# Which PSUM bank the second head's transposed probabilities use, and which head norm starts one block later

## The chip, the cores and the metric

The kernel runs on one core of one Trainium2 chip. The number that counts is the device time of one execution in microseconds (us); smaller is better. Engines are named as in the profile: PE is TensorE (matmuls and transposes), PEld its weight loads, ACT is ScalarE, DVE is VectorE, POOL is GpSimd, SP issues the weight transfers. PSUM, where PE writes its results, has eight banks; a tile here is always one whole bank.

## The reference, cut to what matters

The model is two blocks over 256 tokens of width 1024: an even mixer, an expert layer, an attention layer with 16 heads of 64 (`fox_mix`), a second expert layer, then a second block with a windowed attention of 8 heads (`sliding_window_attention`) and a gated MLP. The change touches the two attentions only.

```
q = rms_norm(q.reshape(B, S, FOX_HEADS, FOX_HD), q_g)     # the head norm; k likewise
k = rms_norm(k.reshape(B, S, FOX_HEADS, FOX_HD), k_g)
...
logits = logits + c[:, :, lo:hi, None] - c[:, :, None, :hi]   # c: cumulated log of the forget gates
probs = jax.nn.softmax(jnp.where(mask, logits, -jnp.inf), axis=-1)
outs.append(jnp.einsum('bhqk,bhkd->bhqd', probs.astype(v.dtype), v[:, :, :hi]))
```

## The kernel before, in words

Each engine executes its instructions in the order in which the program issues them. All weights come as a stream of blocks of 128 x 1024 numbers. SP fetches a block (`w_raw`), ACT makes its high part (`w_hi`, L337), DVE the remainder (`w_lo`, L353), and PE multiplies with both. A weight block is 24 matmuls of 256 columns or 12 of 512.

Small work is woven between the blocks by generators that yield: `flow.step()` advances every active generator by one step, oldest first. In the attention `attend` (L1410) makes one round of it: one step, one weight block, then a new pair of heads is added, then two more steps. `pair_chain` (L1350) is the generator of one pair of heads. Its steps are: logits of head 0 with row maximum and exponential; the same for head 1; division by the row sums (L1384, L1387, which write `pb`); the transposes of head 0's probabilities (`pt`, L1393) and the copy out of PSUM (`pts`, L1395); the same for head 1; an empty step; the product with the values (`po`, L1403); and the split of that product into `y_hi` (ACT) and `y_lo` (DVE, L1406, shown in the trace as L460 and L461; `ya_hi` and `ya_lo` in the second block). Since a new pair starts in every round, three pairs are under way at once. In one round the order on PE is: block, `po` of the oldest pair, head 0's transposes of the middle pair, head 0's logits of the newest, head 1's transposes of the middle pair, head 1's logits of the newest, next block.

The four objects `pj`, `pa`, `pl` and `po` each hand out PSUM banks in turn from a list. While the pairs run the lists are

```
banks((4, 5), (0,), (1, 2), (3,))        # pj, pa, pl, po in fox_mix
banks((4, 5, 6, 7), (0,), (1, 2), (3,))  # in the windowed attention
```

so that `pa` has bank 0 and `po` has bank 3. A tile that is put into a bank waits until the tile before it in that bank has been read.

Ahead of the pairs, while the q and k blocks of `fox_mix` are multiplied, `quad(b)` (L1515) norms four tiles at a time by `rms_heads` (L1314): step 1 sums squares with matmuls of 2 columns (`qn_ps`), takes a root on ACT and an inverse on DVE; steps 2 and 3 spread the result by transposes (`qn_rb`). There are four of these, `quad(0)`, `quad(2)`, `quad(4)` and `quad(6)`. `forget()` (L1448) runs beside them: a projection with 16 outputs (`fz_ps`), then ACT work with three table loads (Exp, Ln, Sqrt), then the sums `c_ps`. A bare `yield` ahead of a quad puts it one weight block later.

Of the kernel before, what the change touches and what calls it, by code (L numbers as in the profile page):

```python
# [378 lines left out]
def body(ctx: ExitStack, tc: tile.TileContext, a, out, phases=(0, 6)):  # L379
# [20 lines left out]
    pj, pa, pl, po = Banks(), Banks(), Banks(), Banks()  # L400
# [26 lines left out]
    def col(name, i=0, n=1):  # L427
        at, w = COLS[name]
        assert i + n <= w
        return cols[:, at + i:at + i + n]  # L430
# [20 lines left out]
    def mm(o, l, r, start, stop):  # L451
        nc.tensor.matmul(o, l, r, start=start, stop=stop, skip_group_check=True)  # L452
# [6 lines left out]
    def split_to(hi, lo, src):  # L459
        nc.scalar.activation(hi, src, AF.Copy)  # L460
        nc.vector.tensor_sub(lo, src, hi.bitcast(F32))  # L461

    def preload(func):

        nc.scalar.activation(scr, epst, func)
# [848 lines left out]
    def rms_heads(qk, qz, sq, items, gains, tp, bd64, bufs=2):  # L1314


        n = len(items)
        ps = pa("qn_ps")
        ind = bd64[:, 0:P:64]
        for i, b in enumerate(items):  # L1320
            for tb in range(2):
                j = 4 * i + 2 * tb
                mm(ps[:, j:j + 2], sq(b)[:, tb * P:(tb + 1) * P], ind, i + tb == 0, True)
        rs = tp.tile([P, 4 * n], F32, name="qn_rs", tag="qn_rs")
        nc.scalar.activation(rs, ps[:, :4 * n], AF.Sqrt, bias=epst, scale=1.0 / 64)
        nc.vector.reciprocal(rs, rs)
        rx = tp.tile([P, 4 * n, 64], F32, name="qn_rx", tag="qn_rx", bufs=bufs)
        nc.scalar.activation(rx, rs.unsqueeze(2).to_broadcast([P, 4 * n, 64]), AF.Copy)
        yield
        for i0 in range(0, n, 2):  # L1330
            m = min(2, n - i0)
            hb = pa("qn_rb")
            for i in range(i0, i0 + m):
                for tb in range(2):
                    j = 4 * i + 2 * tb
                    nc.tensor.transpose(hb[:, ((i - i0) * 2 + tb) * P:((i - i0) * 2 + tb + 1) * P],
                                        rx[:, j:j + 2].rearrange("p a b -> p (a b)"), ident)
            for i in range(i0, i0 + m):
                b = items[i]
                at = slice((i - i0) * S, (i - i0 + 1) * S)  # L1340
                if b >= qz.shape[2]:
                    nc.vector.scalar_tensor_tensor(qk(b), qk(b), gains[i], hb[:, at], op0=OP.mult, op1=OP.mult)
                    continue
                for e in range(2):
                    pr = slice(e * 64, (e + 1) * 64)
                    nc.vector.scalar_tensor_tensor(qz[pr, e, b], qk(b)[pr], gains[i][pr], hb[pr, at],
                                                   op0=OP.mult, op1=OP.mult)
            yield

    def pair_chain(b, heads, tp, qz, kT, y, bias, shift, sink, vcol, vn, ready):  # L1350

        lts, mxs, pbs, ptss = [], [], [], []
        for e, hd in enumerate(heads):
            lg = pl("lg")
            lt = [lg[:, S:S + P], lg[:, 0:S]]
            for tb in (1, 0):
                n = (tb + 1) * P
                mm(lt[tb], qz[:, e, b, tb * P:n], kT[:, 0:n], tb == 1, False)  # L1360
            bias(hd, lg[:, 0:S + P])
            mx = tp.tile([P, 6], F32, name="mx", tag="mx", bufs=6)
            pb = tp.tile([P, 3, P], F32, name="pb", tag="pb", bufs=5)
            pbt = [pb[:, 0], pb[:, 1:3].rearrange("p a b -> p (a b)")]
            sk = sink(hd)
            for tb in range(2):
                nc.vector.tensor_reduce(mx[:, tb:tb + 1], lt[tb], axis=AX.X, op=OP.max, negate=sk is None)
            for tb in range(2):
                m = mx[:, tb:tb + 1]
                if sk is None:  # L1370
                    nc.vector.tensor_scalar(m, m, shift(hd)[tb], shift(hd)[tb], op0=OP.subtract, op1=OP.add)
                else:
                    nc.vector.tensor_scalar(m, m, sk, -1.0, op0=OP.max, op1=OP.mult)
            for tb in range(2):
                nc.scalar.activation(pbt[tb], lt[tb], AF.Exp, bias=mx[:, tb:tb + 1], accum_out=mx[:, 2 + tb:3 + tb])
            if sk is not None:
                nc.scalar.activation(mx[:, 4:6], mx[:, 0:2], AF.Exp, bias=sk)
            mxs.append(mx)
            pbs.append((pb, pbt))
            yield  # L1380
        for mx, (pb, pbt), hd in zip(mxs, pbs, heads):
            if sink(hd) is not None:
                nc.vector.tensor_add(mx[:, 2:4], mx[:, 2:4], mx[:, 4:6])
            nc.vector.reciprocal(mx[:, 2:4], mx[:, 2:4])  # L1384
        for mx, (pb, pbt) in zip(mxs, pbs):
            for tb in range(2):
                nc.vector.tensor_scalar(pbt[tb], pbt[tb], mx[:, 2 + tb:3 + tb], None, op0=OP.mult)  # L1387
        yield
        for e, hd in enumerate(heads):

            pt = (po if e else pa)("pt")
            for j in range(3):
                nc.tensor.transpose(pt[:, j * P:(j + 1) * P], pbs[e][0][:, j], ident)  # L1393
            pts = tp.tile([P, 3, P], F32, name="pts", tag="pts", bufs=4)
            nc.scalar.activation(pts.rearrange("p a b -> p (a b)"), pt[:, :3 * P], AF.Copy)  # L1395
            ptss.append(pts)
            yield
        yield
        ps = po("po")

        for j, (tb, kb) in enumerate(((0, 0), (1, 0), (1, 1))):
            for e, hd in enumerate(heads):
                mm(ps[e * 64:(e + 1) * 64, tb * P:(tb + 1) * P], vn[:, kb, vcol(hd):vcol(hd) + 64],  # L1403
                   ptss[e][:, j], j == 0, j != 1)
        yield
        split_to(y[0][:, b], y[1][:, b], ps[:, :S])  # L1406
        ready.add(b)
        yield
# [16 lines left out]
    def odd():  # L1425
        banks((4, 5, 6, 7), (0, 1, 2, 3))
        with ExitStack() as es:
# [85 lines left out]
            ready = set()  # L1513

            def quad(b):  # L1515
                if b == 0:
                    yield
                yield from rms_heads(lambda b: qk[:, b], qz, lambda b: sq[:, slot(b)], [b, 8 + b, b + 1, 9 + b], [gq, col("odk"), gq, col("odk")], tp, bd64)
                if b == 6:
                    preload(AF.Exp)  # L1520
                    for bb in range(8):
                        pending.append(pair_chain(bb, (2 * bb, 2 * bb + 1), tp, qz, qk[:, 8 + bb], y, bias,
                                                  lambda hd: [cq[:, tb, hd:hd + 1] for tb in range(2)],
                                                  lambda hd: None, lambda hd: hd * 64, vn, ready))

            def qk_out(b, ps):
                nc.vector.tensor_mul(qk[:, b], ps[:, :S], rb)
                nc.scalar.activation(sq[:, slot(b)], qk[:, b], AF.Square)
                if b >= 8 and b % 2:
                    flow.add(quad(b - 9))  # L1530
# [318 lines left out]
```

## Time and profile before

| | |
|---|---|
| three timed runs, median | 2374.05 us (2372.49 to 2374.91) |
| profiled execution, its own time | 2373.32 us |
| its span in the profile | 2371.5 us |
| PE busy | 2316.3 us, 98% of the span |
| PE clock granted, mean over the span | 0.991 of full speed |
| DVE, ACT busy | 73%, 57% |
| mean memory traffic | 163 GB/s |

PE is busy nearly all of the time, so what PE waits for is what can be won or lost; the few slices of the page in which PE falls below 9 tenths are the stages with attention. Its busy time also holds stretches in which its clock was granted at half.

### The profile page before, as it was taken

Reading aid. Unit: us, or ns where it says so; the run is one execution under the profiler, and the core shown is the slowest. Engines: PE = TensorE matmul, PEld = TensorE weight load, DVE = VectorE, ACT = ScalarE, POOL = GpSimd, SP = SyncE. Lnnn points to the kernel's source line nnn. Section 1 sums busy time; section 2 is a strip of 40 time slices with the busy share of each in tenths; the row PEclk is TensorE's granted clock in tenths of the full one; section 3 lists DMA queues with packets and bytes.
Section 4 is the critical chain, followed back from the end, with each engine's and each line's share of the span. In section 5 each row is a group of like instructions: output and inputs, shape, how many; then the busy total and the mean of one; then the engine's idle time right before and its main releaser. Section 6 shows DMA issues by size and latency. Waiting matters only on the chain. (4 is left out here: it accounts for less than half of the span.)

```text
span 2371.5 us, 48790 instructions
## 1 busy us (share of the span) xinstructions
PE 2316.3 (98%) x19664; PEld 2267.2 (96%) x19664; DVE 1723.1 (73%) x3656; ACT 1361.4 (57%) x2488; POOL 81.1 (3%) x99
## 2 busy tenths in 40 slices
PE   8999999999999999998899999999999999989999
PEld 7889999999999999997799999999999999989999
DVE  6768989999655555555489899996555555657983
ACT  6236448888544444555464588885444445555762
POOL 4100000000000000000000000000000000000200
PEclk9999999999999999999999999999999999999999
DMA  6125654444566666552155554445556565645563
GB/s 212 54 67 179 194 185 152 146 146 140 184 187 184 203 185 186 169 185 96 48 169 194 180 156 146 143 143 184 184 187 203 186 187 161 213 126 173 180 185 124
DMA packets 106627, 386.82 MB, mean 163 GB/s; under 512 B 11960, under 2 KB 13273, under 8 KB 106017
## 3 DMA queue, kind: packets, MB, share of 16 engines
q1 hardware_dynamic: 104976, 377.99, 50.6%
q0 software_dynamic: 1136, 5.32, 0.7%
q8 instruction: 154, 2.52, 0.4%
q14 instruction: 73, 0.59, 0.1%
q10 hardware_dynamic: 288, 0.40, 0.1%
HBM read 383.40 MB, written 1.05 MB: 162 GB/s over the span
## 5 line engine op out<-in xcount | busy, mean ns | idle before, releaser
L353 DVE TENSOR_TENSOR w_lo<-w_raw,w_hi 128x1024 fp32r<-128x1024 f32 x710 | 866.1, 1224 | 383.7 <-ACT w_hi L337 382.2
L337 ACT ACTIVATE w_hi<-w_raw 128x1024 fp32r<-128x1024 f32 x710 | 745.7, 1054 | 433.9 <-PE pv L452 348.6
L452 PE MATMUL pu<-h_hi,w_hi 128*128 128x256 f32 x2048 | 586.8, 287 | 0.0
L452 PE MATMUL pu<-h_lo,w_hi 128*128 128x256 f32 x2048 | 575.2, 281 | 0.0
L452 PE MATMUL pu<-h_hi,w_lo 128*128 128x256 f32 x2048 | 574.6, 281 | 0.0
L452 PE MATMUL pv<-h_hi,w_hi 128*128 128x256 f32 x1888 | 530.4, 281 | 0.0
L452 PE MATMUL pv<-h_lo,w_hi 128*128 128x256 f32 x1888 | 530.4, 281 | 0.0
L452 PE MATMUL pv<-h_hi,w_lo 128*128 128x256 f32 x1888 | 530.4, 281 | 0.0
L452 PEld LDWEIGHTS pu<-h_lo,w_hi 128*128 128x128 f32 x2048 | 386.4, 189 | 0.0
L452 PEld LDWEIGHTS pu<-h_hi,w_lo 128*128 128x128 f32 x2048 | 385.7, 188 | 0.0
L452 PEld LDWEIGHTS pu<-h_hi,w_hi 128*128 128x128 f32 x2048 | 385.5, 188 | 0.0
L452 PEld LDWEIGHTS pv<-h_hi,w_lo 128*128 128x128 f32 x1888 | 355.8, 188 | 0.0
L452 PEld LDWEIGHTS pv<-h_lo,w_hi 128*128 128x128 f32 x1888 | 355.8, 188 | 0.0
L452 PEld LDWEIGHTS pv<-h_hi,w_hi 128*128 128x128 f32 x1888 | 355.8, 188 | 0.0
L1271 ACT ACTIVATE X<-pu 128x256 f32<-128x256 f32 (+31 forms) x228 | 74.3, 326 | 197.0 <-PE pu L452 197.0
L1168 ACT ACTIVATE oa<-cb,routed 128x128 bf16<-128x128 f32 x512 | 162.9, 398 | 0.0
L1173 DVE TENSOR_TENSOR ob<-ob,g 128x512 bf16<-128x512 bf16 x256 | 108.0, 422 | 4.4
L452 PEld LDWEIGHTS <-oa 128*128 128x128 bf16 x1536 | 90.2, 96 | 12.9 <-issue 5.3
L452 PE MATMUL g<-ob,oa 128*128 128x128 bf16 x1024 | 102.1, 219 | 0.0
L452 PE MATMUL g<-oa 128*128 128x128 bf16 x512 | 94.7, 219 | 0.3
L461 DVE TENSOR_TENSOR h_lo<-X,h_hi 128x512 fp32r<-128x512 f32 (+1 forms) x134 | 86.4, 653 | 2.1 <-ACT h_hi L460 1.9
L1174 ACT ACTIVATE oa<-oa 128x512 bf16<-128x512 bf16 x128 | 80.8, 631 | 4.1
(450 smaller groups left out, 4111.6 us busy)
## 6 DMA issues: line engine op xcount, KB each, us to landing
w_raw<-in_s_u SPq DMA_DIRECT2D x256, 512.0 KB, 3.5
w_raw<-in_s_v SPq DMA_DIRECT2D x256, 512.0 KB, 4.3
w_raw<-in_s_mix SPq DMA_DIRECT2D x46, 512.0 KB, 3.7
w_raw<-in_s_up SPq DMA_DIRECT2D x44, 512.0 KB, 4.3
w_raw<-in_s_wq SPq DMA_DIRECT2D x32, 512.0 KB, 3.8
w_raw<-in_s_odd SPq DMA_DIRECT2D x32, 512.0 KB, 4.2
w_raw<-in_s_even SPq DMA_DIRECT2D x28, 512.0 KB, 3.8
w_raw<-in_s_down SPq DMA_DIRECT2D x22, 512.0 KB, 4.3
```

The costliest lines, as they stand in the source:

```text
L337: self.nc.scalar.activation(hi, raw, AF.Copy)
L353: self.nc.vector.tensor_sub(lo, raw, hi.bitcast(F32))
L452: nc.tensor.matmul(o, l, r, start=start, stop=stop, skip_group_check=True)
L461: nc.vector.tensor_sub(lo, src, hi.bitcast(F32))
L1168: nc.scalar.activation(o[0][:, i * P:(i + 1) * P], iota, AF.Abs, bias=ne1T[:, t0 + i:t0 + i + 1])
L1173: nc.vector.tensor_tensor(two[part], two[2], pairs(g3[:, part, t0:t0 + GT]), op=OP.mult)
L1174: nc.scalar.activation(o[0], o[0], AF.Relu, bias=1.0, scale=-1.0)
L1271: nc.scalar.activation(X(c)[:, td:], ps[:, td:S], AF.Gelu)
```

## The change

First part: head 1's transposes take their bank from `pa` (bank 0), as head 0's do, and no longer from `po` (bank 3), which the products of the pairs use. Second part: the bare `yield` is moved from `quad(0)` to `quad(2)`, so `quad(0)` starts one weight block earlier and `quad(2)` one later. `quad(4)` and `quad(6)` stay.

```
         for e, hd in enumerate(heads):
-
-            pt = (po if e else pa)("pt")
+            pt = pa("pt")
             for j in range(3):
                 nc.tensor.transpose(pt[:, j * P:(j + 1) * P], pbs[e][0][:, j], ident)
             pts = tp.tile([P, 3, P], F32, name="pts", tag="pts", bufs=4)
...
             def quad(b):
-                if b == 0:
+                if b == 2:
                     yield
                 yield from rms_heads(lambda b: qk[:, b], qz, lambda b: sq[:, slot(b)], [b, 8 + b, b + 1, 9 + b], [gq, col("odk"), gq, col("odk")], tp, bd64)
```

Line numbers behind the first hunk are lower by one in the changed kernel. On PE the order within a round of pairs is the same; what each instruction waits for is not. This is the difference on PE in the third round of `fox_mix`'s attention, from the end of the logits of the newest pair's head 0 into those of its head 1 (`lg` are logits, `pt` the transposes of the middle pair's head 1; the names in brackets are the engines waited for):

```order
 L452 LDWEIGHTS identb
 L452 MATMUL lg<-causalb,identb 128x256
-L1393 MATMUL pt<-cb,pb 128x128 [waits DVE_49,PE_49]
-L1393 MATMUL pt<-cb,pb 128x128 x2
-L452 MATMUL lg<-qk,qz 128x256 [waits Activation_49]
+L1392 MATMUL pt<-cb,pb 128x128 [waits DVE_49,Activation_49]
+L1392 MATMUL pt<-cb,pb 128x128 [waits DVE_49]
+L1392 MATMUL pt<-cb,pb 128x128
+L452 MATMUL lg<-qk,qz 128x256
 L452 MATMUL lg<-qk,qz 128x128
 L452 MATMUL lg<-nck,sel 128x384
```

The transposes stood behind a DVE instruction, the `y_lo` that empties bank 3, and now stand behind an ACT instruction, the copy `pts` that empties bank 0.

The second part moves whole steps. On ACT, at `quad(0)` (`qk_sq` are squares, `qn_rs` and `qn_rx` the root of the quad and its spreading, `fzT` belongs to `forget()`), the rows of before are

```order
L1528 ACTIVATE qk_sq<-qk 128x256
L337 ACTIVATE w_hi<-w_raw 128x1024
L1457 ACTIVATE fzT<-fz_ps 16x256
L1325 ACTIVATE qn_rs<-qn_ps,epst 128x16
L1328 ACTIVATE qn_rx<-qn_rs 128x1024
```

and those of the change

```order
L1527 ACTIVATE qk_sq<-qk 128x256
L337 ACTIVATE w_hi<-w_raw 128x1024
L1325 ACTIVATE qn_rs<-qn_ps,epst 128x16
L1328 ACTIVATE qn_rx<-qn_rs 128x1024
L1527 ACTIVATE qk_sq<-qk 128x256
```

so the root of `quad(0)` now comes one pair of squares and weight block sooner and ahead of `fzT`. At `quad(2)`, behind the last two table loads of `forget()`, the rows of before are

```order
L1470 ACT_TABLE_LOAD
L1470 ACTIVATE fzab<-fzab 128x32
L465 ACT_TABLE_LOAD
L465 ACTIVATE scr<-epst 128x1
L1528 ACTIVATE qk_sq<-qk 128x256
L337 ACTIVATE w_hi<-w_raw 128x1024
L1325 ACTIVATE qn_rs<-qn_ps,epst 128x16
L1328 ACTIVATE qn_rx<-qn_rs 128x1024
```

and those of the change

```order
L465 ACT_TABLE_LOAD
L465 ACTIVATE scr<-epst 128x1
L1527 ACTIVATE qk_sq<-qk 128x256
L337 ACTIVATE w_hi<-w_raw 128x1024
L1527 ACTIVATE qk_sq<-qk 128x256
L337 ACTIVATE w_hi<-w_raw 128x1024
L1476 ACTIVATE sel<-qz 128x1024
L1325 ACTIVATE qn_rs<-qn_ps,epst 128x16
L1328 ACTIVATE qn_rx<-qn_rs 128x1024
```

so one more square, one more weight block and a copy of `forget()` stand between the table loads and the root of `quad(2)`. On PE the matmuls of 2 columns move by the same one block.

## Rows read from the trace of the kernel before

**Rows 1.** PE's waits around the two attentions: us in total, times, longest.

```profile
PE pt L1393 <- DVE y_lo L461: 17.7, 7, 2.7
PE pt L1393 <- DVE ya_lo L461: 6.4, 3, 2.9
```

**Rows 2.** Timeline of fox_mix's pairs: start us, us, engine, line, operation [idle before <-releaser].

```profile
1089.64 0.49 PE L1393 MATMUL pt<-cb,pb 128*128 128x128 f32 x3
...
1095.89 0.55 PE L1393 MATMUL pt<-cb,pb 128*128 128x128 f32 x3
1096.47 0.49 ACT L1395 ACTIVATE pts<-pt 128x384 f32<-128x384 f32 x1 [1.30 <-PE pt L1393]
...
1097.43 0.62 DVE L1367 TENSOR_REDUCE mx<-lg 128x1 f32<-128x128 f32 x2 [0.97 <-PE lg L452]
...
1099.55 0.42 DVE L461 TENSOR_TENSOR y_lo<-po,y_hi 128x256 fp32r<-128x256 f32 x1 [1.13 <-ACT y_hi L460]
1100.12 0.52 PE L1393 MATMUL pt<-cb,pb 128*128 128x128 f32 x3 [2.73 <-DVE y_lo L461]
...
1101.63 0.62 DVE L1367 TENSOR_REDUCE mx<-lg 128x1 f32<-128x128 f32 x2 [1.66 <-PE lg L452]
...
1103.34 1.05 ACT L337 ACTIVATE w_hi<-w_raw 128x1024 fp32r<-128x1024 f32 x1
1103.55 0.99 DVE L1387 TENSOR_SCALAR pb<-pb,mx 128x128 f32<-128x128 f32 x4
...
1104.46 1.22 DVE L353 TENSOR_TENSOR w_lo<-w_raw,w_hi 128x1024 fp32r<-128x1024 f32 x1
```

**Rows 3.** Timeline, the last pair of fox_mix.

```profile
1160.29 0.55 PE L1393 MATMUL pt<-cb,pb 128*128 128x128 f32 x3
...
1162.21 0.55 PE L1393 MATMUL pt<-cb,pb 128*128 128x128 f32 x3 [1.37 <-DVE y_lo L461]
```

**Rows 4.** Stretches: busy us (instructions) of PE, PEld, DVE, ACT, POOL; PE clock; DMA.

```profile
1095.90:1160.30 64.40, 48.03 (x315) 41.73 (x313) 27.98 (x97) 24.41 (x73) 0.00 (x0) 0.84 0.11 33
1040.00:1046.00 6.00, 6.00 (x40) 6.00 (x40) 2.34 (x5) 4.07 (x6) 0.00 (x0) 0.72 0.31 100
...
1086.00:1095.90 9.90, 9.90 (x62) 7.90 (x60) 7.91 (x30) 6.42 (x20) 0.00 (x0) 1.00 0.25 90
```

**Rows 5.** Timeline of the windowed attention's pairs.

```profile
2078.96 0.55 PE L1393 MATMUL pt<-cb,pb 128*128 128x128 f32 x3
...
2089.78 0.62 DVE L1367 TENSOR_REDUCE mx<-lg 128x1 f32<-128x128 f32 x2 [0.22 <-PE lg L452]
...
2092.02 0.42 DVE L461 TENSOR_TENSOR ya_lo<-po,ya_hi 128x256 fp32r<-128x256 f32 x1 [1.37 <-ACT ya_hi L460]
...
2095.11 0.62 DVE L1367 TENSOR_REDUCE mx<-lg 128x1 f32<-128x128 f32 x2 [2.66 <-PE lg L452]
...
2097.35 0.99 DVE L1387 TENSOR_SCALAR pb<-pb,mx 128x128 f32<-128x128 f32 x4
...
2098.59 1.22 DVE L353 TENSOR_TENSOR w_lo<-w_raw,w_hi 128x1024 fp32r<-128x1024 f32 x1
2098.79 0.55 PE L1393 MATMUL pt<-cb,pb 128*128 128x128 f32 x3
```

**Rows 6.** Timeline at quad(2): ACT's last table load, and PE's matmuls of 2 columns.

```profile
1037.90 1.28 ACT L465 ACT_TABLE_LOAD   x1
...
1039.75 0.61 PE L452 MATMUL qn_ps<-masks,qk_sq 128*128 128x2 f32 x4 [1.14 <-ACT qk_sq L1528]
```

**Rows 7.** Timeline ahead of quad(0): the transfer of the masks, the last square, the projection's end.

```profile
1012.63 0.56 POOL L423 DMA_DIRECT2D masks<-in_c_masks  x1
...
1018.78 0.42 ACT L1528 ACTIVATE qk_sq<-qk 128x256 f32<-128x256 f32 x1 [0.69 <-DVE qk L1527]
...
1022.85 0.28 PE L452 MATMUL fz_ps<-h_hi,fws_l 128*16 128x256 f32 x1
```

**Rows 8.** The tile of the masks: from the issue of its transfer to its landing.

```profile
DMA to landing us min/median/max: 9.8/9.8/9.8
```

More of the change, by code (lines that the diff above doesn't have):

```diff
@@ L1389, in pair_chain @@
         for e, hd in enumerate(heads):
-            pt = (po if e else pa)("pt")
+            pt = pa("pt")
             for j in range(3):
@@ L1515, in quad @@
             def quad(b):
-                if b == 0:
+                if b == 2:
                     yield
```

## The prediction

> **What bounds the kernel now.** I read the view of waits first, for PE in the two stretches that the change touches, since PE is busy for 98% of the span and only its gaps and its clock can give time back. One wait stands out [rows 1]: head 1's transposes wait for `y_lo` 7 times in `fox_mix` (17.7 us) and for `ya_lo` 3 times in the windowed attention (6.4 us). The timeline of one round says why [rows 2]: PE could take head 1's transposes when the logits of the newest pair's head 0 are done, which DVE's row maximum marks at 1097.43, but starts them at 1100.12 after an idle of 2.73. They go into bank 3, which holds the oldest pair's product, and this is emptied only when `y_lo` ends at 1099.97. `y_lo` is late because ACT does the newest pair's exponentials ahead of `y_hi`, and they need the row maximum first.
>
> The view of stretches shows a second loss [rows 4]. From the first round with such a wait to the last pair, 64.4 us, PE is busy for 48.03 only, and the mean granted clock is 0.84 of full. [...] Before the waits begin it is 1.00. The only idle of this size in these rounds is the wait, and I take the clock's fall as its consequence.
>
> The third place is `quad(2)`: PE waits 1.14 us for a square that ACT makes only after its table loads [rows 6], and then the clock is 0.72 over 6 us [rows 4].
>
> **The change, part by part.** Nothing is added on any engine: the same instructions run, 12 groups of three transposes wait for something else, and two quads move by one block.
>
> *Bank, fox_mix.* A round from one pair's head 0 transposes to the next pair's is 6.25 us without the wait (1089.64 to 1095.89, PE never idle, clock 1.00 [rows 2, 4]). The next six, 1095.89 to 1160.29, take 64.4 us, 10.73 each [rows 2, 3]. What is a round when the wait is gone? PE needs 6.25. The other candidate is the ring of dependences on DVE, which is the thing that is late next. With each leg from its row [rows 2]:
> - head 0's row maximum, exponentials, `y_hi`, to the start of `y_lo`: 1099.55 - 1097.43 = 2.12;
> - `y_lo`: 0.42. It stays ahead of head 1's row maximum in DVE's order, so it stays in the ring;
> - head 1's row maximum, exponentials, to the division: 1103.55 - 1101.63 = 1.92;
> - the division and the `w_lo` behind it: 1104.46 + 1.22 - 1103.55 = 2.13, then DVE is free for the next row maximum.
>
> That is 6.59, a little over PE's 6.25. PE would idle for 0.3 at the next pair's head 0 transposes. I take 6.59, since both are floors and the larger one binds. Six rounds: 64.4 - 6 x 6.59 = 24.9 us.
>
> The new wait is for `pts`, the copy of head 0 out of bank 0. It starts 0.58 after the transposes start and takes 0.49, so it is over at 1096.96, while PE is on the newest pair's head 0 logits until about 1097.4 [rows 2]. Its lower bound is therefore nothing. The upper one is a `w_hi` (1.05) in front of the copy on ACT with the copy itself (0.49) exposed, 1.54 a round. In a round of 6.59 `w_hi` starts 0.21 ahead of the division (1103.34 against 1103.55) and ends 0.84 behind it; the copy ends at 1.33 then, and the row maximum starts only at 2.13, when `w_lo` ends. So I take nothing and keep 1.54 for the range.
>
> Head 1's logits and their bank wait for nothing new: their exponentials were read a round ago. Bank 3 now serves the products alone and is free long before the next one. Behind the waiting transposes on PE stand head 1's logits and the next weight block; whatever they waited, the block waited too, so the gain is one to one.
>
> *Bank, last pair.* There is no newer pair, so the copy is not covered: head 1's transposes can start 0.58 + 0.49 after head 0's plus the hop of 0.15 from an end to PE's start (1099.97 to 1100.12 [rows 2]), 1161.51 instead of 1162.21 [rows 3]. Gain 0.7.
>
> *Bank, windowed attention.* Two rounds, 2078.96 to 2098.79, take 19.83 [rows 5]. The same ring: 2092.02 - 2089.78 = 2.24, `ya_lo` 0.42, 2097.35 - 2095.11 = 2.24, and from the division to the end of `w_lo`, with a tile of the gates between them, 2098.59 + 1.22 - 2097.35 = 2.46; together 7.36. Gain 19.83 - 14.72 = 5.1, and 0.7 at the last pair as above. The first pair has no wait now and none later.
>
> *The quads.* `quad(2)` one block later: ACT's last table load ends at 1039.18 and the missing square soon behind it, so PE has a whole weight block of other work by then; the wait of 1.14 goes, and with it the clock's loss, 6.00 x (1 - 0.72) = 1.7 [rows 4, 6]. Gain 2.8. `quad(0)` one block earlier follows the `forget()` projection, whose last matmul starts at 1022.85. Its last square was made at 1018.78, and the masks, fetched by POOL's queue at 1012.63, land 9.8 later, at 1022.43 [rows 7, 8]. So it has 0.4 us to spare on the transfer, and costs nothing. The root on ACT and the inverse on DVE run ahead of `fzT`, whose reader on PE comes two blocks later, so that is covered; without this cover it would be the one copy of 16 rows, under 0.5 by its neighbour `pts`. Weights are split two blocks ahead, so a quicker PE does not meet them.
>
> Sum: 24.9 + 0.7 + 5.1 + 0.7 + 2.8 = 34.2. The profiled execution's own time is 2373.3, so 2339.1; the median of the timed runs is 0.7 above it, which I leave to the range.
>
> [...] In the trace the copy out of bank 0 is over before PE wants the bank again [rows 2]. [...]
>
> **The rivals.**
> - *The wait moves to bank 0.* The copy `pts` is late because ACT is behind with `w_hi`. Price: 1.54 in eight rounds, 12.3, so 2351.4. For it: rounds get shorter and ACT's work does not. Against it: ACT is busy for 24.41 of 64.4 us [rows 4], and the margin above. Chance 0.10.
> - *The wait goes, the clock stays at 0.84.* A round is then 6.25 / 0.84 = 7.44, 0.85 over the ring, in eight rounds 6.8; with the 1.7 at `quad(2)` not won, 2347.6. For it: the clock fell in the quad where the wait was only 1.14. Against: 1.00 in the round without a wait. Chance 0.08.
> - *The quads turn against us.* The masks land late, or the clock now falls at `quad(0)`, because `fz_ps` with its 16 outputs and the matmuls of 2 columns stand back to back. Price: nothing won, and a loss of the size of today's at `quad(2)`, 2.8: 2344.7. Chance 0.11.
> - *Slower: half clock throughout.* The short idles that are left come in every round, and the clock never gets back to full. At half a round takes 12.5 against 10.73: 6 x 1.77 = 10.6 more, in the other attention 2 x 12.5 - 19.83 = 5.2 more, less 2.8: 2386.3. It decides when the mean clock in the rounds is under 6.25 / 10.73 = 0.58. Against it: 1.00 with PE busy throughout [rows 4]. [...] Chance 0.03.
> - *No change,* because head 1's transposes wait for something else that ends as late as `y_lo`. Rows 2 show nothing such: their probabilities are ready before head 0's transposes end. Chance 0.02.
>
> **How the numbers follow.** The forecast has 0.66. Its own spread is small: PE alone binding (6.25) would give 2.7 more in eight rounds, 2336.4. With that for the lower end, a little below it, and the first rival for the upper, 2335.5 to 2351.5 takes in the forecast, most of the second, third and first rivals, and leaves out about 0.15. A difference under 0.2% (4.7 us) can't be told from no change; faster than that is everything but the last two rivals, 0.95; same 0.02; slower 0.03.
>
> **What would show it.** The waits of `pt` for `y_lo` and `ya_lo` are gone; `po` to `po` about 6.6 and 7.4; the clock near 1.00 from the second pair on; a small wait, if any, of head 0's transposes for the division on DVE; no wait at `qn_ps`. I am wrong if `pt` waits for `pts` by a microsecond or more, if the clock stays low in rounds without idle, or if the time that the attention gives back reappears as a wait for weights in the expert layer behind it.

## The result, and the profile after

The changed kernel takes 2338.09 us (median of five runs, 2335.78 to 2338.72), the kernel before 2373.18 beside it (five runs, 2369.67 to 2374.91): a ratio of 0.9851, interval 0.9836 to 0.9865. It is faster, by 35.1 us. The profiled run took 2338.51 with a span of 2336.7.

PE's waits in the stretch of `fox_mix`, which answer to [rows 1]: us in total, times, longest.

```profile
PE pt L1392 <- ACT pts L1394: 1.1, 2, 0.6
PE qk_ps L452 <- DVE h_lo L486: 0.3, 1, 0.3
PE pt L1392 <- DVE pb L1387: 0.2, 1, 0.2
```

And in the windowed attention:

```profile
PE pt L1392 <- ACT pts L1394: 1.4, 2, 0.8
PE pt L1392 <- DVE pb L1387: 0.7, 1, 0.7
```

The waits for `y_lo` and `ya_lo`, 24.1 us in all, are gone. 3.4 us at `pt` have come instead, 2.5 of it for the copy out of bank 0. The timeline of two rounds in `fox_mix`, and the last pair behind them, answers to [rows 2, 3]:

```profile
1094.68 0.55 PE L1392 MATMUL pt<-cb,pb 128*128 128x128 f32 x3
...
1095.26 0.49 ACT L1394 ACTIVATE pts<-pt 128x384 f32<-128x384 f32 x1 [1.30 <-PE pt L1392]
...
1096.02 0.49 PE L1392 MATMUL pt<-cb,pb 128*128 128x128 f32 x3
...
1096.22 0.62 DVE L1367 TENSOR_REDUCE mx<-lg 128x1 f32<-128x128 f32 x2 [0.97 <-PE lg L452]
...
1098.34 0.42 DVE L461 TENSOR_TENSOR y_lo<-po,y_hi 128x256 fp32r<-128x256 f32 x1 [1.13 <-ACT y_hi L460]
1098.68 0.61 DVE L1367 TENSOR_REDUCE mx<-lg 128x1 f32<-128x128 f32 x2
...
1100.60 0.99 DVE L1387 TENSOR_SCALAR pb<-pb,mx 128x128 f32<-128x128 f32 x4
1101.01 0.61 PE L1392 MATMUL pt<-cb,pb 128*128 128x128 f32 x3
...
1101.33 1.26 ACT L1547 ACTIVATE vn<-va,rs 128x512 f32<-128x512 f32 x2
...
1102.47 0.50 ACT L1394 ACTIVATE pts<-pt 128x384 f32<-128x384 f32 x1
...
1102.64 0.62 DVE L1367 TENSOR_REDUCE mx<-lg 128x1 f32<-128x128 f32 x2
...
1103.03 0.55 PE L1392 MATMUL pt<-cb,pb 128*128 128x128 f32 x3 [0.45 <-ACT pts L1394]
...
1133.98 0.61 PE L1392 MATMUL pt<-cb,pb 128*128 128x128 f32 x3 [0.23 <-DVE pb L1387]
...
1135.23 0.55 PE L1392 MATMUL pt<-cb,pb 128*128 128x128 f32 x3 [0.64 <-ACT pts L1394]
```

In the first round the copy of head 0 is over at 1095.75 and PE takes the bank at 1096.02: a margin of 0.27. In the second, two copies of the values (`vn`, 1.26 us) stand ahead of `pts` on ACT, and PE waits 0.45. In the last pair there is nothing to cover the copy, and head 1 starts 1.25 behind head 0, where it was 1.92 [rows 3].

The stretches answer to [rows 4]. First the six rounds, then `quad(2)`, then what is left behind `quad(4)`; columns as there.

```profile
1094.70:1134.00 39.30, 38.63 (x315) 34.01 (x313) 25.99 (x94) 23.65 (x73) 0.00 (x0) 1.00 0.18 54
...
1040.00:1046.00 6.00, 6.00 (x54) 6.00 (x52) 2.62 (x5) 5.67 (x9) 0.00 (x0) 1.00 0.40 126
1056.00:1058.00 2.00, 2.00 (x12) 2.00 (x13) 1.44 (x3) 1.43 (x3) 0.00 (x0) 0.57 0.04 16
1058.00:1060.00 2.00, 2.00 (x12) 2.00 (x12) 0.64 (x3) 1.66 (x4) 0.00 (x0) 0.57 0.27 61
```

The six rounds take 39.30 us in place of 64.4; PE idles for 0.67 of it and its granted clock is 1.00 over the stretch. At `quad(2)` the clock has gone from 0.72 to 1.00. A fall to 0.57 is left behind `quad(4)`; before had one there too (0.50 from 1058 to 1060).

In the windowed attention (answering to [rows 5]) the first pair has a wait that it did not have:

```profile
2042.99 0.55 PE L1392 MATMUL pt<-cb,pb 128*128 128x128 f32 x3
...
2043.85 0.42 DVE L1669 TENSOR_TENSOR su<-mx_ps,su 128x256 f32<-128x256 f32 x1
...
2044.30 0.42 ACT L1670 ACTIVATE yg_hi<-su 128x256 fp32r<-128x256 f32 x1 [2.18 <-DVE su L1669]
2044.63 0.47 ACT L1394 ACTIVATE pts<-pt 128x384 f32<-128x384 f32 x1
...
2045.15 0.55 PE L1392 MATMUL pt<-cb,pb 128*128 128x128 f32 x3 [0.79 <-ACT pts L1394]
...
2051.31 0.55 PE L1392 MATMUL pt<-cb,pb 128*128 128x128 f32 x3
...
2065.43 0.61 PE L1392 MATMUL pt<-cb,pb 128*128 128x128 f32 x3 [0.70 <-DVE pb L1387]
```

The copy starts 1.64 behind the transposes, since ACT issues `yg_hi` ahead of it, and that waits for DVE. The two rounds behind it take 14.12 (2051.31 to 2065.43), before 19.83.

By stage, each from one event on PE to the same event in the other kernel:

| stage | before | after |
|---|---|---|
| quads: from the attention layer's `n_rb` to the first logits | 70.63 | 68.06 |
| attention layer: from its `n_rb` to the next layer's | 169.79 | 141.45 |
| expert layer: from that `n_rb` to the next | 836.04 | 835.96 |
| windowed attention: from that `n_rb` to the last `po` | 83.87 | 76.83 |

The gains are 28.34 and 7.04, together 35.4 (the first row is part of the second). Of the 7.04, 1.6 comes from a fall of the clock that is in the one trace and not in the other, ahead of the pairs and in code that is the same; the part on the prediction takes this up. Nothing is given back in the expert layer between them. Stages are compared below rather than totals where they can be, since the attention layer begins at 1012.8 to 1020.5 in these traces, by work ahead of it that no kernel here changes.

### The profile page after: what moved, and what is told of

Same layout as the page of the kernel before. It is cut to its first block, busy times and chain, and to the rows that moved or that the text cites. A ratio compares the mean times of both kernels' runs of the same rounds, so it can differ in the third digit from the quotient of the medians.

```text
span 2336.7 us, 48804 instructions
## 1 busy us (share of the span) xinstructions
PE 2303.7 (99%) x19664; PEld 2256.5 (97%) x19664; DVE 1721.6 (74%) x3656; ACT 1360.1 (58%) x2488; POOL 81.0 (3%) x99
```

## The experiments

**Theory A**, that of the prediction: head 1's transposes wait because bank 3 is emptied late, by a split that DVE does behind the newest pair's row maximum and exponentials; the idle of 2.73 in each round also takes the clock down; sharing bank 0 costs nothing because its copy is over in time. **Rivals:** that sharing or not sharing a bank is what matters and not when it is emptied; that the clock falls in the rounds for a reason of its own; that the quads bring the gain.

**The bank part alone.** On the kernel before:

```
-            pt = (po if e else pa)("pt")
+            pt = pa("pt")
```

> The kernel before with the first part of the change alone: head 1's transposes in bank 0, the quads as before. If the time came from the wait for the split in bank 3 and from the clock that fell behind it, nearly all of the gain is here: 31.4 us by the sum of the prediction (24.9 + 0.7 + 5.1 + 0.7), a median near 2342 us, rounds of about 6.4 us, clock 1.00 in the rounds, and the wait of 1.1 us at the second quad still there with the low clock behind it. If the quads had given more than their 2.8 us, or if the parts needed each other, the gain here is under 28 us.

Measured: 2339.48 (2338.73 to 2340.4), ratio 0.9865, interval 0.9848 to 0.9882. The six rounds take 39.28, the attention layer 144.03, the quads 70.67 with the old wait at `quad(2)`. So the bank is nearly all of the change.

**The quads alone.** On the kernel before:

```
             def quad(b):
-                if b == 0:
+                if b == 2:
                     yield
```

> The kernel before with the second part alone: the second quad one weight block later, the first one earlier, head 1's transposes in bank 3. By the sum 2.8 us: a median near 2370.4 us, no wait at the quad's matmuls of 2 columns, clock 1.00 from 1040 to 1046 us, and the rounds of the attention as slow as before (10.7 us). If the earlier first quad costs what the later second one gives, the time is that of before and a wait or a low clock stands at the first quad.

Measured: 2368.67 (2361.74 to 2372.01, 12 runs), ratio 0.9983, interval 0.9973 to 0.9994. The quads take 68.18, 2.45 less. The wait in the rounds stays as it was:

```profile
PE pt L1393 <- DVE y_lo L461: 17.7, 7, 2.7
```

Against 2372.2 of before beside them (17 runs) the one part gains 32.7 and the other 3.5, together 36.3 against 35.1 for both. Within the scatter the two parts add up.

**Bank 3 kept, but emptied early.** On the kernel before, the split of a pair's product is issued directly behind the product, with no step between:

```
                    ptss[e][:, j], j == 0, j != 1)
-        yield
         split_to(y[0][:, b], y[1][:, b], ps[:, :S])
```

> The kernel before, banks and quads as they were, but the split of the product (y_hi on ACT, y_lo on DVE) is issued directly behind the product instead of one step later, so it stands ahead of the newest pair's exponentials. If the cause is that bank 3 is emptied late, because the split stands behind exponentials, this alone takes the wait away as the bank did: rounds of 6.3 to 6.6 us, clock 1.00, a median of 2340 to 2344 us. If it is the sharing of bank 3 as such (a transpose behind a product in one bank), or a hazard of PE on its own writes, the wait stays and the median stays above 2365 us.

Measured: 2338.26 (2337.51 to 2344.24), ratio 0.986, interval 0.9843 to 0.9876. Its waits at `pt` in `fox_mix`, its stretch of six rounds, and DVE's row of events in one of them:

```profile
PE pt L1393 <- DVE y_lo L461: 0.6, 1, 0.6
```

```profile
1100.40:1138.60 38.20, 38.20 (x314) 33.94 (x312) 27.77 (x97) 24.19 (x73) 0.00 (x0) 1.00 0.19 56
```

```profile
1100.92 0.42 DVE L461 TENSOR_TENSOR y_lo<-po,y_hi 128x256 fp32r<-128x256 f32 x1
1101.93 0.62 DVE L1367 TENSOR_REDUCE mx<-lg 128x1 f32<-128x128 f32 x2 [0.58 <-PE lg L452]
```

The same bank for the same two tenants, and no wait in the rounds (the 0.6 is the last pair's): `y_lo` is now over before the row maximum. What cost the time was the late emptying and not the bank. PE never idles in these rounds, which take 6.37 each; that is PE's own work. In the windowed attention two waits for `ya_lo` are left, 1.3 together, 1.1 of it the last pair's; the first pair has none.

**A shorter idle.** On the kernel before, head 1's transposes come one step later, behind more of PE's work, and still go into bank 3:

```
         for e, hd in enumerate(heads):
-
+            if e:
+                yield
             pt = (po if e else pa)("pt")
...
-        yield
         ps = po("po")
```

> The kernel before, with head 1's transposes one step later, behind the newest pair's head 1 logits, still in bank 3 (the empty step that stood behind them is dropped, so the product comes when it did). PE's wait for y_lo shrinks by the logits that now run ahead of it, from 2.7 to about 1.7 us a round. If the clock falls only behind the long idle, a round is 6.25 + 1.7 = 7.9 us, the clock 1.00 and the gain some 20 us (near 2353 us). If the clock falls at this idle as well, a round is 9.3 to 9.6 us at a mean clock near 0.85 and the gain is about 10 us (near 2363 us). If the low clock has nothing to do with the idle but with the mix of matmuls in a round, it is as low as before.

Measured: 2355.79 (2353.81 to 2359.51), ratio 0.994, interval 0.9922 to 0.9958. Its wait and its stretch of rounds:

```profile
PE pt L1394 <- DVE y_lo L461: 12.0, 7, 1.8
```

```profile
1093.80:1143.80 50.00, 39.38 (x314) 34.14 (x312) 27.75 (x97) 23.72 (x73) 0.00 (x0) 1.00 0.14 43
```

With an idle of 1.77 in every round the clock stays at full; with 2.73 it was 0.84 in before, and 0.91 in the six rounds of the run with the quads alone:

```profile
1094.20:1154.40 60.20, 43.83 (x316) 37.85 (x313) 28.25 (x97) 24.42 (x73) 0.00 (x0) 0.91 0.12 36
```

This divides the loss. The 64.40 us of before are 16.37 of idle and 48.03 of PE busy, against 38.20 in the rounds without idle. The rounds of this run, at full clock but with an idle in each, have PE busy for 39.38; so 1.2 of the difference comes with the interruptions themselves, and 8.65 is the clock's. In the run with the quads alone the clock's part by the same reckoning is 4.4: the wait is the same in each of the six rounds, but the clock fell in three of them there and in five in before, each time within a microsecond of the wait's end. That the clock falls in the rounds for a reason of its own is not borne out: in none of the runs with rounds of short or no idle did it fall there. But a wait of 2.73 does not always bring a fall.

In the windowed attention of this run a single idle of 2.03 was followed by a fall, in the second of the two rounds:

```profile
2061.20:2079.60 18.40, 15.25 (x122) 13.31 (x121) 11.07 (x41) 8.87 (x29) 0.00 (x0) 0.91 0.21 60
```

**The change with the early split as well.** On the changed kernel, the same edit as above.

> The changed kernel with the split of the product issued directly behind the product. It takes y_hi and y_lo out of the ring of dependences (0.42 us by their leg) and ahead of the copy. If PE itself binds the rounds at 6.3 us, little is left: the six rounds of the first attention go from 39.3 us to 38 at best, and the stage from one norm to the next from 141.5 to about 140.5. If the ring on DVE binds them, as the prediction had it, they fall by 0.3 us each, to 37.5.

Measured in a single run: 2335.46; the six rounds 38.22, without a wait, the attention layer 139.89. A round is 6.37 on the mean, against 6.55 in the changed kernel. Nearly all of the 1.08 between the two sums lies in two rounds, the one with the `vn` copies ahead of `pts` (7.12, here 6.39) and the last, with its wait of 0.23 for DVE's division (6.70, here 6.37); the other four take as long in both kernels, within 0.03. At `quad(0)` a wait that the prediction had held possible turned up:

```profile
1023.70 1.95 PE L452 MATMUL qn_ps<-masks,qk_sq 128*128 128x2 f32 x16 [0.79 <-DMA masks<-in_c_masks]
```

**quad(4) one block later too.** On the changed kernel, `if b in (2, 4):` in place of `if b == 2:`.

> The changed kernel with the third quad (quad(4)) one block later too, so that its matmuls of 2 columns no longer follow the sums c_ps directly. Before and after the change the clock was near 0.57 for four us behind this place, with PE never idle. If the run of narrow matmuls makes the clock fall, a weight block between them keeps it at 1.00 and the quads get 1.7 us shorter (68.1 to 66.4 from the norm's broadcast to the first logits). If it is chance where the clock falls, nothing changes, or it falls elsewhere.

Measured in a single run: 2338.08; the quads 66.61 in place of 68.06, the clock 1.00 over the whole stage, the attention layer 140.01. The stage is 1.4 shorter; the total, within the scatter of single runs, does not show it. That the delay of `quad(4)` is what took the fall away is not shown: in the run with the early split, where `quad(4)` is not delayed, the clock did not fall there either (the quads 67.64, with 0.79 of it the wait for the masks).

**No quad delayed.** On the changed kernel:

```
             def quad(b):
-                if b == 2:
-                    yield
```

> The changed kernel without the bare yield: the first quad stays one block earlier and the second is back where it was. If the second part's gain is all from the second quad being later, and the earlier first quad costs and gives nothing, the quads take as long as with the bank change alone (70.7 us from the norm's broadcast to the first logits), with the wait of 1.1 us at the second quad. If the earlier first quad gave part of the gain, they take 69 to 70 us without a wait.

Measured in a single run: 2341.72; the quads 71.12, with a wait of 1.6 and a fall of the clock behind it, shown in three stretches:

```profile
PE qn_ps L452 <- ACT qk_sq L1525: 1.6, 1, 1.6
```

```profile
1042.00:1044.00 2.00, 2.00 (x15) 2.00 (x15) 1.12 (x3) 1.68 (x3) 0.00 (x0) 0.75 0.00 0
1044.00:1046.00 2.00, 2.00 (x11) 2.00 (x11) 0.54 (x1) 2.00 (x4) 0.00 (x0) 0.50 0.25 49
1046.00:1048.00 2.00, 2.00 (x18) 2.00 (x17) 0.64 (x2) 0.42 (x1) 0.00 (x0) 0.89 0.62 213
```

Against before (70.63) it has only `quad(0)` earlier, and gains nothing in the stage; against the change (68.06) it lacks only the delay of `quad(2)`, and loses 3.1. Part of the 3.1 is scatter: the stage took 68.06 in the changed kernel's first trace and 69.72 in its second, where the fall behind `quad(4)` lasted longer:

```profile
1020.50:1090.20 69.70, 69.66 (x510) 65.75 (x509) 41.53 (x74) 39.84 (x62) 1.80 (x1) 0.95 0.52 180
```

What holds in every trace is the part at `quad(2)`. The five kernels that do not delay it have the wait there (1.14, here 1.58) with a fall of the clock behind it (with the bank part alone by its mean of 0.94 from 1024 to 1084, that of before); the seven traces of kernels that delay it have neither. So the gain, as far as it is more than scatter, is that of `quad(2)`.

**The copy doubled.** On the changed kernel each copy of the transposes is made twice, so bank 0 comes free 0.5 later:

```
-            nc.scalar.activation(pts.rearrange("p a b -> p (a b)"), pt[:, :3 * P], AF.Copy)
+            for _ in range(2):
+                nc.scalar.activation(pts.rearrange("p a b -> p (a b)"), pt[:, :3 * P], AF.Copy)
```

> The changed kernel with each copy of the transposes out of PSUM made twice (the second writes the same again): 0.49 us more on ACT for each of 24 copies. It measures how far the first rival (the wait moves to bank 0) is. The copy ends some 0.27 us before PE wants the bank. If this margin is what separates the kernel from that rival, PE now waits for the copy by 0.2 us in each round, the copy of head 1 delays its exponentials by as much again, and a round goes from 6.4 to 6.7 to 7.0 us, 2.5 to 5 us in all eight. If ACT's copies are far from the path, the time stays within 1 us.

Measured in a single run: 2346.91, of which 4.9 is a later start of the attention layer. Its PE rows of two rounds:

```profile
1106.58 0.55 PE L1392 MATMUL pt<-cb,pb 128*128 128x128 f32 x3
1108.76 0.55 PE L1392 MATMUL pt<-cb,pb 128*128 128x128 f32 x3 [0.67 <-ACT pts L1395]
1113.86 0.55 PE L1392 MATMUL pt<-cb,pb 128*128 128x128 f32 x3
1115.51 0.55 PE L1392 MATMUL pt<-cb,pb 128*128 128x128 f32 x3
```

Head 1 now follows head 0 by 1.65 instead of 1.34, so of the 0.5 added 0.3 is seen and 0.2 was margin. The six rounds take 40.95, the attention layer 143.88, 2.4 more; the windowed attention 77.79, 0.96 more, all of it in its first and last pair. The mechanism of the first rival of the prediction is real and stood this close, but its size is small.

**All of it.** The changed kernel with the early split, `quad(4)` later as well, and the masks fetched ahead of the selection matrices (1024 KB) on POOL's queue:

```
+            upper, bd64, causal = masks(sp, 0, 3)
             nc.gpsimd.dma_start(self32, a["c_sel"].rearrange("p (h t) -> p h t", h=16))
-            upper, bd64, causal = masks(sp, 0, 3)
...
-                if b == 2:
+                if b in (2, 4):
...
                    ptss[e][:, j], j == 0, j != 1)
-        yield
         split_to(y[0][:, b], y[1][:, b], ps[:, :S])
```

> The change, with three things more that the runs so far point to: the split of a pair's product is issued directly behind the product (no step between them), quad(4) too starts one weight block later, and the masks are fetched ahead of the 16 selection matrices. Theory A (what was left after the change is a ring on DVE that is about as long as PE's own round, a fall of the clock behind the 2-column matmuls of quad(4), and a transfer of the masks with 0.4 us of margin; the three are independent): a round of fox_mix's pairs 6.37 as with the early split alone, the quads stage 66.6 as with quad(4) later alone and no wait of qn_ps for the masks, from one n_rb broadcast of the attention layer to the next about 138.5 (141.45 in the change), total about 3 us or 0.13% under the change. Rival B (what one part wins another loses: the earlier quads only meet a wait for something else): the stage stays at 139.9 or more and the total at 2335.5 or more.

and beside it the changed kernel once more:

> The changed kernel unaltered, on the same chip as the version with the three additions, so that the two can be compared. Both theories: 2338.1 as before, ratio to the kernel before 0.985.

Measured: 2334.16 (2332.48 to 2337.59, five runs), ratio to before 0.9843, interval 0.9825 to 0.986; the changed kernel on the same chip 2338.15 (2335.74 to 2344.38, four runs), ratio 0.9856, interval 0.9836 to 0.9876. The attention layer takes 138.84 (143.08 in the changed kernel's trace of this chip, 141.45 in its first), the quads 66.61, the six rounds 38.22:

```profile
1096.40:1134.60 38.20, 38.20 (x314) 33.96 (x312) 27.77 (x97) 24.18 (x73) 0.00 (x0) 1.00 0.18 56
```

The masks' transfer, median from issue to landing in the last column, in this kernel and then in the changed kernel's first trace (9.9 in the run with `quad(4)` later):

```profile
masks<-in_c_masks POOLq DMA_DIRECT2D x1, 192.0 KB, 5.8
```

```profile
masks<-in_c_masks POOLq DMA_DIRECT2D x1, 192.0 KB, 10.2
```

It is 4.0 below the changed kernel by the medians, but the ranges and the intervals overlap, so the totals do not yet tell the two versions apart. The rounds and the masks' transfer show two of the additions at work; for `quad(4)` the caution above stands.

## Why the prediction was right

**The size.** 2339.1 was forecast from a sum of 34.2; 2338.09 was measured, and 34.8 between the two profiled runs. Right on the total and on the mechanism: the wait for the late split went, the clock came back with it, and bank 0 was free in time in all but a few places. Beneath the total several steps were off, and their errors partly cancel; that it came out within 1 us is in part luck.

**Bank, `fox_mix`.** Forecast 24.9, measured 25.1 (64.4 to 39.30). The wait and the clock's loss went together, as argued. The ring is where it was put: `mx` to `mx` is 1102.64 - 1096.22 = 6.42 on DVE, without an idle ahead of the second. It is 0.17 under the 6.59 of the sum, because two DVE instructions in succession overlap by nearly 0.1 in the records (`y_lo` ends at 1098.76, the row maximum behind it starts at 1098.68) and whole durations were added up. PE's own round is 6.37 and not the 6.25 taken from a single round. So both candidates lie within 0.05 of each other, and the step by which the ring binds each round, with PE idle for 0.3 in it, is not what happened: PE waited for the division once in six rounds, for 0.23. Four rounds take 6.33 to 6.41, PE's own time. What brought the mean to 6.55, close to the 6.59, is the last round of 6.70 and one of 7.12, with the `vn` copies ahead of `pts`. That is luck.

**"I take nothing and keep 1.54 for the range."** That was the step on the copy `pts`, and it holds in the rounds but for that one. Only `w_hi` was looked at as what ACT might have in hand; the `vn` copies, once in the six rounds, were overlooked, and cost a wait of 0.45. They stand in the trace of before too, right behind the `w_hi` that was priced:

```profile
1104.29 1.26 ACT L1548 ACTIVATE vn<-va,rs 128x512 f32<-128x512 f32 x2
```

**Last pair.** 0.7 forecast, 1.92 - 1.25 = 0.67 measured, in either attention nearly the same.

**"The first pair has no wait now and none later."** This step of the part on the windowed attention failed. The row was there in the trace of before and was not read; PE's transposes of the first pair and ACT's copy:

```profile
2071.65 0.55 PE L1393 MATMUL pt<-cb,pb 128*128 128x128 f32 x3
...
2072.85 0.49 PE L1393 MATMUL pt<-cb,pb 128*128 128x128 f32 x3
```

```profile
2073.29 0.47 ACT L1395 ACTIVATE pts<-pt 128x384 f32<-128x384 f32 x1
```

Head 0's copy ended at 2073.76, and head 1's transposes had begun 0.91 before, because they had a bank of their own. With one bank that becomes a delay: 0.91 and the hop of 0.15 would have given 1.06, and the pair's round went from 7.31 to 8.32, 1.01 more. The two later rounds made up for 0.6 of it: 5.71 gained instead of 5.1 (14.12 instead of 14.72). They take 7.24 and 6.88 (the second starts at 2058.55), and not 7.36 each: DVE held PE back only in the second, by 0.70 at the division, and even there its ring, from division to division, measures 7.18 (2057.84 to 2065.02). Net of both and the last pair 5.36, against 5.8; the kernel with the bank part alone gained 5.37 in this stage. The changed kernel gained 7.04, and 1.60 of the rest lies ahead of the pairs, where the code is the same. In before the clock was at half behind the matmuls of 2 columns that open this stage, and in after it was not. This was no part of the forecast, and it hides the first pair's loss in the total. First before, then after:

```profile
2034.00:2037.00 3.00, 3.00 (x8) 2.38 (x9) 1.35 (x2) 2.53 (x4) 0.00 (x0) 0.50 0.78 220
```

```profile
2006.90:2009.90 3.00, 3.00 (x16) 2.45 (x16) 1.35 (x2) 2.49 (x4) 0.00 (x0) 1.00 0.69 218
```

**The quads.** 2.8 forecast; 2.57 in the change, 2.45 with the quads alone, but only 0.91 by the changed kernel's second trace (70.63 to 69.72). The wait of 1.14 and the fall at `quad(2)` went as forecast; the 1.7 for the clock is not certain, since the clock fell behind `quad(4)` as well, for about 3 us in the changed kernel's first trace and 6 in its second (by matmuls that took over 0.39 in place of 0.28). That `quad(0)` costs nothing held in the change, where it is the masks that decide: in the changed kernel they were issued at 1013.98 and landed 10.2 later, at 1024.18, and the matmuls that read them start at 1024.32, without an idle. The margin is about 0.1, not 0.4; in the run with the early split it was missed, at a transfer of 11.2, and cost 0.79. Fetching the masks first took the transfer to 5.8 in the one trace of it, well clear of the wait.

**One bank or two.** Sharing a bank won 32.7 us over going to a second one that is emptied late; a second one with an early split (38.20 of 38.20 us busy) is, in the six rounds, as good as sharing with one (38.22). So a bank of its own does not by itself put the emptying beside other matmuls: with the late split PE stood for 2.73 in each of the six rounds, with the early one in none. What counted in these runs is when the bank's last reader got its turn.

**The rivals.** *The wait moves to bank 0*: 2.5 us of waits in place of the 12.3 priced, real where nothing covers the copy or ACT has something ahead of it. *The clock stays low*, *half clock throughout*: 1.00 in the rounds, with idles of 0.2 to 0.45 left. No run shows the 12.5 of the last, a round at half from end to end: the lowest mean measured over the six is 0.84, in before. *The quads turn against us*: once, for 0.79. *No change*: excluded, since the waits for `y_lo` and `ya_lo` are gone and the time with them.

## What to carry to other kernels

Before giving two uses separate PSUM banks, read who empties each bank and what stands ahead of that reader on its engine: here an early copy had the shared bank free 0.27 us before it was wanted, in a round with work to cover it, and a late split held PE up by 2.73 at a separate one. When a buffer becomes shared, look up the end of its last reader against the next writer's start in every round and in both places where the code runs, the first and the last round too; each wait for the copy in the changed kernel could be read off the old trace this way. Where one wait is long, count with the clock as well as with the idle time: here 8.65 of the 26.2 us lost in the six rounds were clock in one trace, and about 4.4 of 22 in another.

## What the runs showed of the hardware

The granted clock fell in eight of twelve rounds with one idle of 2.73 us (five of six in before, three of six with the quads alone; in before to 0.50, as from 1110 to 1112 and from 1120 to 1126; with the quads alone the three transposes behind the wait took 0.87 in place of 0.52), each time within a microsecond of the idle's end, and in none of six rounds with one of 1.77 (1.00 over all six), of the same instructions with head 1's transposes one group of logits later. In the windowed attention it fell behind an idle of 2.03 in the run with the shorter idle (0.91 over the stretch shown there), and not behind one of 2.13 in before (1.00 from 2080 to 2089). So in these runs the length of the idle alone does not tell whether the clock falls.

With the matmuls of 2 columns a shorter idle had a fall behind it. At `quad(2)` that is so in all five traces with a wait of 1.14 or 1.58 (0.72 over 6 us in before, 0.50 from 1044 to 1046 with no quad delayed), and the seven without the wait have none.

Falls behind matmuls of 2 columns without a wait are not the same in each run of the same code. The changed kernel's quads had a mean clock of 0.97 in one trace and 0.95 in another (68.06 and 69.72 us). The fall that opens the windowed attention (matmuls of 512 columns at 0.63 each in before, 0.39 in after) came in six of the ten traces that show the stretch: in before and, of the kernels with the whole change in them, with the early split and with `quad(4)` later, but not in after. Whether the change has a part in that, and what decides it, is open. It puts an uncertainty of 1 to 2 us on each total, about the size of the quads' gain.
